# Start addresses of the on-chip buffers in a two-layer grid encoder: column buffers in a pool of their own, constants padded

## The chip, the core and the metric

The kernel runs on one core of a Trainium2 chip. A core has five engines with instruction streams of their own: TensorE (PE; its weight loads are shown as PEld), VectorE (DVE), ScalarE (ACT), GpSimd (POOL) and SyncE (SP), which here issues the transfers. The metric is the device time of one execution in microseconds; lower is better.

## The reference

An encoder trunk of two layers over 512 tokens (a grid of 8 x 64) of 1,024 features, with 256 memory tokens:

```
for l in range(2):
    h = rms_norm(x, norm_mix[l])
    x = x + (even_mixer(h) if l == 0 else odd_mixer(h))
    x = x + memory_cross_attention(rms_norm(x), rms_norm(mem))
    x = x + conv_ffn(rms_norm(x))          # 1024 -> 2 x 2816 -> 1024
```

The even mixer is grouped-query attention and a two-way mLSTM behind one input projection and one output projection; the odd mixer is neighbourhood attention and differential attention in the same form. The feed-forward part projects up, applies a convolution over three positions and a gate, and projects down. Everything is in fp32.

## The kernel before

Activations lie transposed: a tile holds 128 features (rows) by 512 tokens (columns). To keep the precision of fp32 each operand is split into a rounded part and a rest, `hi` and `lo`, both in a rounded fp32 format (fp32r), and a product is made of three matmuls (`mm3`): w_hi x h_hi, w_hi x h_lo, w_lo x h_hi. `gemm` runs these three for each of the eight blocks of 128 features. Weights come in chunks of 128 x 1024: `stage` transfers a chunk into a buffer of class st, and `weights` splits it into a buffer of class w (hi in the first half, lo in the second). In `gemm` the weights are the stationary operand (128 columns) and a tile of activations is the moving one (512 columns). In `tok_gemm`, which makes rows of tokens, it is the other way about: the activations are stationary, and the moving operand is 512 columns of w. Attention products and transposes are in plain fp32.

Instructions are recorded first (`Recorder.add`) and then ordered by a list schedule (`Recorder.schedule`) from costs in the source; it also gives each buffer a slot of its class (`SLOTS`): 80 of class a (512 floats in each partition), 4 of st (1,024), 3 of w (2,048), 48 of c (8 floats: the columns of a few numbers for each partition) and 8 banks p for sums. `Recorder.trace` issues the instructions in that order, which is why nearly every row of the profile names line 391. The schedule knows slots by number only and no addresses.

A slot gets its place in memory when a pool meets its tag for the first time; a pool lays its tiles one behind the other, each at the next multiple of 32 bytes. Constants lie in the pool "const", ahead of the pool "slots", which holds a, st, w and c mixed in the order of their first use. In the program as built:

- The constants ones, ones64, ident, identr and vec start 32 bytes past a multiple of 128, because eps ahead of them takes 4 bytes.
- a0 to a60, all st and all w start 64 bytes past a multiple of 128.
- c0 (32 bytes) was first used after a60 and before a61, and so a61 to a79 start 96 bytes past a multiple of 128. The other c follow at the end.

Within a buffer all matmul operands start at multiples of 512 bytes, so they keep these remainders. 5,419 matmuls are of 512 columns in fp32r: 1,200 of them have a moving operand at 96, all others at 64.

How slot numbers are read: the names below are slot, number of the buffer and number of the instruction that first wrote it. These are TensorE's rows in the middle of one block of the first layer's up projection, destination first, then moving and stationary operand. Of the slots in them a72, a69, a66, a79 are at 96 and a20 and w0 at 64.

```order
L391 MATMUL p1_3121_4153<-a72_2578_3503,w0_3056_4077 128x512
L391 MATMUL p1_3121_4153<-a69_2586_3514,w0_3056_4077 128x512
L391 MATMUL p1_3121_4153<-a72_2578_3503,w0_3056_4077 128x512
L391 MATMUL p1_3121_4153<-a66_2594_3524,w0_3056_4077 128x512
L391 MATMUL p1_3121_4153<-a79_2603_3536,w0_3056_4077 128x512
L391 MATMUL p1_3121_4153<-a66_2594_3524,w0_3056_4077 128x512
L391 MATMUL p1_3121_4153<-a20_2616_3551,w0_3056_4077 128x512
```

The next block begins with a26, a43, a26, a44, a60, a44, a24 against w1, all at 64.

Of the kernel before, what the change touches and what calls it, by code (L numbers as in the profile page):

```python
# [11 lines left out]
F32 = mybir.dt.float32  # L12
# [13 lines left out]
SLOTS = {"a": (80, 512), "st": (4, 1024), "w": (3, 2048), "c": (48, 8), "p": (8, 512)}  # L26
# [24 lines left out]
NVEC = _vec_layout()  # L51


class Buf:
    """A buffer of one slot class; the slot is chosen when the schedule is made."""

# [5 lines left out]
class View:  # L62
    """A recorded view of a Buf; resolved to an access pattern when its instruction is traced."""

# [23 lines left out]
    def grid(self, pattern, i):  # L88
        """[p, n] as [p, i, n/i] ("p (i c) -> p i c") or, of columns in the other order, "p (c i) -> p i c"."""
        p, n = self.dummy.shape  # L90
        return View(self.buf, self.ops + (("grid", (pattern, i)),), np.broadcast_to(np.int8(0), (p, i, n // i)))

    def spread(self, n):
        """[p, m] as [p, m, n], each element n times."""
        p, m = self.dummy.shape
        return View(self.buf, self.ops + (("spread", n),), np.broadcast_to(np.int8(0), (p, m, n)))
# [17 lines left out]
class Op:  # L114
    """An instruction: alts holds (engine, method, args, keywords, cost, latency) for each engine that may run it."""

# [20 lines left out]
class Recorder:  # L137
    """Records instructions with their buffers, orders them by a list schedule, then traces them in that order."""

# [97 lines left out]
    def schedule(self, slots):  # L237
        """List schedule: each engine takes, of the instructions that are ready, the first in program order. A
        buffer is given one of its class's slots with its first write and gives it back after its last use."""
        import heapq  # L240
# [153 lines left out]
class Kern:  # L394
# [33 lines left out]
    def finish(self):  # L428
        tc = self.tc
        pool = lambda name, **kw: self.ctx.enter_context(tc.tile_pool(name=name, bufs=1, **kw))  # L430
        sb, ps = pool("slots"), pool("banks", space=bass.MemoryType.PSUM)
        rec = self.nc
        rec.trace(rec.schedule({c: n for c, (n, w) in SLOTS.items()}),
                  lambda cls: (ps if cls == "p" else sb, SLOTS[cls][1]))

# [11 lines left out]
    def rest(self, lo, src, hi, gain=None, rows=slice(None)):  # L447
        """lo: what scaled_copy's rounding left of src * gain."""
        if gain is None:
            self.nc.vector.tensor_tensor(lo, src, hi.bitcast(F32), op=OP.subtract)  # L450
        else:
            self.nc.vector.scalar_tensor_tensor(lo, src, gain[rows], hi.bitcast(F32), op0=OP.mult, op1=OP.subtract)
# [58 lines left out]
class Norm:  # L511
# [29 lines left out]
    def columns(self):  # L541
        """rstd, and its square, of token 128 * t + p in row p of columns t and 4 + t."""
        K, nt = self.K, self.n // 128
        nc = K.nc
        p = K.ps("t")[:, :32 * nt]
        for t in range(nt):
            nc.tensor.transpose(p[:, 32 * t:32 * t + 32], self.r[0:32, t * 128:t * 128 + 128], K.ident[0:32, 0:32])
        self.rc = K.col("rc")
        nc.vector.tensor_copy(self.rc[:, :nt].grid(ROWS, nt), p.grid(ROWS, nt)[:, :, 0:1])
        nc.vector.tensor_tensor(self.rc[:, 4:4 + nt], self.rc[:, :nt], self.rc[:, :nt], op=OP.mult)  # L550
# [16 lines left out]
def softmax(K, sc, n, bias=None):  # L567
    """exp(sc - max) and 1 / its sum, of sc and of a bias added to it."""
    nc = K.nc
    c = K.col("sm")  # L570
    P = K.a("P")[:, :n]
    if bias is None:
        nc.vector.tensor_reduce(c[:, 0:1], sc, op=OP.max, axis=AX.X, negate=True)
        nc.scalar.activation(P, sc, AF.Exp, bias=c[:, 0:1], accum_out=c[:, 1:2])
    else:
        nc.vector.tensor_tensor_reduce(P, sc, bias, -1.0, 3.0e38, op0=OP.add, op1=OP.min, accum_out=c[:, 0:1])
        nc.scalar.activation(P, P, AF.Exp, bias=c[:, 0:1], scale=-1.0, accum_out=c[:, 1:2])
    nc.vector.reciprocal(c[:, 2:3], c[:, 1:2])
    return P, c[:, 2:3]


class Head:
    """One head, or two (parts) of 64 columns each: score(i, part) -> P of query tile i, finish(Ps) -> P tiles by part,
    v(kt) -> the stationary operands of key block kt by part, take(y)."""

# [71 lines left out]
def merge(main, fill, name, rest=True):  # L657
    """Emit main, with fill's work spread through it (ratio of PE time), and then what is left of fill (rest)."""
    debt, ratio = TUNE[name + "0"], TUNE[name]
    for c in main:  # L660
        debt += c * ratio
        while fill is not None and debt > 0:
            try:
                debt -= next(fill)
            except StopIteration:
                fill = None
        yield c
    if rest and fill is not None:
        yield from fill
# [12 lines left out]
def q_stack(K, q, gain=None):  # L682
    """Two heads' [hi; lo] rows: [qa_hi; qa_lo] and [qb_lo; qb_hi]."""
    lo, hi = slice(0, 64), slice(64, 128)
    qa, qb = K.ar("qa"), K.ar("qb")
    for t, src, dst in ((qa, lo, hi), (qb, hi, lo)):
        K.scaled_copy(t[src], q[src], gain, src)
        K.rest(t[dst], q[src], t[src], gain, src)
    return qa, qb


def k_stack(K, k, gain=None):
    """What the stacked q is multiplied with, of two heads: hi against both its halves, lo against its hi half."""
    nc = K.nc
# [12 lines left out]
def scores2(K, q2, k2, i, keys=None):  # L707
    """Query tile i against all keys, or against two key tiles."""
    nc = K.nc
# [14 lines left out]
def trunk(ctx, tc, xT, memT, vec, lam_in, rope, ev_w, ev_o, od_w, od_o, ca_q, ca_kv, ca_o, up, down, na_u, t5, outT):  # L724
# [3 lines left out]
    real = tc.nc  # L728
    eps = pc.tile([128, 1], F32, name="eps")
    real.vector.memset(eps, EPS)  # L730
# [17 lines left out]
    x, w0 = [], []  # L748
    V, mix = K.const(pc.tile([128, NVEC], F32, name="vec")), K.const(pc.tile([128, 8], F32, name="mix"))
    nc.sync.dma_start(mix, vec[:, :8])  # L750
# [41 lines left out]
    def tok_gemm(w, nrm, width):  # L792
        """Token rows times `width` columns of a matrix: a bank holds 512 // width blocks of 128 tokens."""
        kp, per = 1024 // width, 512 // width
# [18 lines left out]
    class Tok:  # L813
        """Token rows: groups of `width` columns, each a list of banks."""

# [8 lines left out]
    def tok_values(w, nrm, v, roll=False):  # L824
        """Values, each token row times its rstd; roll: row n goes to row n + 64."""
        width, per = v.width, 512 // v.width
# [15 lines left out]
    def tok_norm(w, nrm, width, refine):  # L842
        """Token rows, rms_norm over each head of 64, but for its gain. A list of transposed 128-column chunks."""
        per, nh = 512 // width, width // 64
# [25 lines left out]
    def tok_heads(w, nrm, width, gain, refine, stack, roll=False):  # L870
        """Heads of 64 with their gain, transposed and stacked; roll: token n goes to column n + 64."""
        per = 512 // width
# [22 lines left out]
    def proj_norm(w, m, nrm, ones, gain, n=S, d=64, refine=False):  # L895
        """rms_norm over each head of (h * nrm.r) @ w: scale free but for eps, which becomes eps / nrm.r ** 2.
        refine: a Newton step on the root, which turns its sign; gain is negated for it."""
        p = K.ps("g")[:, :n]
        yield from K.gemm(p, w[m], nrm.hs)
        with nc.boosted("qk"):  # L900
            return norm_bank(p, nrm, ones, gain, n, d, refine)
# [240 lines left out]
    def diff(st, ys):  # L1142
        lm = K.a("lm")
        nc.sync.dma_start(lm[:, 0:256], bass.AP(tensor=lam_in.tensor, offset=lam_in.offset, ap=[[0, 128], [1, 256]]))
        lc = K.const(pc.tile([128, 8], F32, name="lam"))
        for j in range(2):
# [34 lines left out]
    def na(st, ys):  # L1181
        """A tile of 128 tokens is 16 grid columns. Keys are turned by 8 columns, so that the windows of query tile i
        lie in key tiles i and i + 1; the last tile's follows on the first, whose halves are at the grid's two ends."""
        def pair(j):
# [22 lines left out]
    def mem_norm(l):  # L1207
        """The memory times a layer's gain; its rstd is the same for both layers."""
        nm = Norm(K, vcol("mem", 8 * l, 8), 256)
# [247 lines left out]
def _rows(yT):  # L1457
    """The output's columns are tokens in column-major order of the grid."""
    return np.ascontiguousarray(yT.reshape(D, 64, 8).transpose(2, 1, 0)).reshape(1, S, D)
# [15 lines left out]
```

## Time and profile before

| | |
|---|---|
| median of 3 runs | 1453.91 us (1449.54 to 1457.04) |
| span of the profiled execution | 1447.9 us; the profile gives no other time of it |
| PE, matmuls | 1430.4 us busy, 6463 records |
| PE, weight loads | 1130.6 us busy |
| VectorE, ScalarE | 966.4 us, 760.4 us busy |
| queue q1 (all transfers) | 29.3% of 16 engines |

The span runs from the first to the last instruction; the time of a run also holds what lies ahead of it and behind it. A matmul's bar is longer than its share of the time, since matmuls overlap in the array: what one costs is the length of a stretch without gaps, divided by the weight loads in it (one for each matmul).

### The profile page before, as it was taken

To read this page: it belongs to the slowest core of one execution; us is meant where nothing else is said; L and a number is where in the kernel's file an instruction comes from. 1 tells how busy PE (TensorE), PEld (TensorE's weight loads), DVE (VectorE), ACT (ScalarE), POOL (GpSimd) and SP (SyncE) were. 2 spreads that over 40 slices of the span, in tenths; PEclk is the share of its full clock that TensorE was granted. 3 is DMA by queue.
4 is the path that set the end of the run, shared out by engine and by line. 5 is a ranking of instruction groups with operands and counts; after the bars stand their busy time and mean duration, and the time that the engine had idled before them with its cause. 6 is when DMAs were issued, how large, how long until landed. Compare 5 with 4: busy or idle time off the path is not lost. (4 is left out here: it accounts for less than half of the span.)

```text
span 1447.9 us, 17456 instructions
## 1 busy us (share of the span) xinstructions
PE 1430.4 (99%) x6463; PEld 1130.6 (78%) x6463; DVE 966.4 (67%) x1744; ACT 760.4 (53%) x1334; POOL 24.0 (2%) x60
## 2 busy tenths in 40 slices
PE   8999999999999999999999999999999999999998
PEld 5787777786888888888888767877778888888887
DVE  7885587666867776733458797857568777776221
ACT  6575697667444444422346777866754444443111
POOL 0000011000000000000000000000000000000000
PEclk9999999999999999999999999999999999999999
DMA  6221221231232333333252402433213332322421
GB/s 235 73 73 59 66 80 56 79 118 45 88 101 90 100 90 100 88 95 97 86 197 67 138 30 88 154 95 107 76 58 90 100 96 94 99 91 66 142 95 48
DMA packets 48182, 135.70 MB, mean 94 GB/s; under 512 B 5473, under 2 KB 12129, under 8 KB 48097
## 3 DMA queue, kind: packets, MB, share of 16 engines
q1 hardware_dynamic: 48096, 134.60, 29.3%
q8 instruction: 50, 0.82, 0.2%
q14 instruction: 36, 0.29, 0.1%
HBM read 132.48 MB, written 2.10 MB: 93 GB/s over the span
## 5 line engine op out<-in xcount | busy, mean ns | idle before, releaser
L391 PE MATMUL p<-a,w 128*128 128x512 f32 (+1 forms) x4560 | 1067.8, 390 | 0.5 <-DVE w L391 0.5
L391 PEld LDWEIGHTS p<-a,w 128*128 128x128 f32 x4560 | 840.7, 188 | 198.1 <-issue 14.6
L391 DVE TENSOR_TENSOR w<-st,w 128x1024 fp32r<-128x1024 f32 (+2 forms) x246 | 279.3, 1136 | 160.7 <-ACT w L391 160.0
L391 ACT CAST w<-st 128x1024 fp32r<-128x1024 f32 (+2 forms) x219 | 213.6, 977 | 247.9 <-PE p L391 221.8
L391 PE MATMUL p<-w,a 128*128 128x512 f32 x768 | 202.2, 402 | 0.9 <-DVE w L391 0.6
L391 DVE SCALAR_TENSOR_TENSOR a<-a,vec,a 128x504 f32<-128x504 f32 (+3 forms) x324 | 183.3, 590 | 11.6 <-ACT a L391 7.5
L391 DVE TENSOR_TENSOR a<-a,a 128x512 fp32r<-128x512 f32 (+5 forms) x215 | 143.4, 670 | 37.5 <-ACT a L391 34.2
L391 PEld LDWEIGHTS p<-w,a 128*128 128x128 f32 x768 | 140.8, 188 | 35.3 <-issue 5.9
L391 DVE TENSOR_TENSOR a<-p,a 128x512 f32<-128x512 f32 (+2 forms) x127 | 85.4, 673 | 108.3 <-PE p L391 82.2
L391 ACT ACTIVATE a<-a 128x512 f32<-128x512 f32 (+2 forms) x170 | 100.7, 600 | 102.3 <-DVE a L391 101.1
L391 PE MATMUL p<-a,a 128*128 128x512 f32 (+1 forms) x424 | 135.0, 432 | 6.6 <-ACT a L391 5.6
L391 ACT CAST a<-a 128x512 fp32r<-128x512 f32 (+2 forms) x92 | 55.9, 608 | 149.3 <-DVE a L391 148.4
L391 ACT ACTIVATE a<-a,vec 128x512 f32<-128x512 f32 (+2 forms) x139 | 105.8, 764 | 43.0 <-DVE a L391 41.4
L391 ACT ACTIVATE a<-a,c 128x256 f32<-128x256 f32 (+3 forms) x172 | 98.4, 598 | 19.6 <-DVE c L391 19.2
L391 PEld LDWEIGHTS p<-a,a 128*128 128x128 f32 x424 | 76.3, 191 | 31.9 <-ACT a L391 10.0
L391 DVE TENSOR_TENSOR a<-a,p 128x512 f32<-128x512 f32 (+1 forms) x65 | 47.9, 738 | 58.4 <-PE p L391 58.4
L391 PEld LDWEIGHTS p<-ident,a 128*128 128x128 f32 (+2 forms) x474 | 55.5, 140 | 26.4 <-DVE a L391 7.3
L391 PE MATMUL p<-ident,a 128*128 128x128 f32 (+2 forms) x474 | 70.0, 273 | 4.2 <-DVE a L391 3.5
L391 ACT COPY a<-p 128x512 f32<-128x512 f32 (+1 forms) x121 | 61.0, 536 | 18.0 <-PE p L391 17.6
L391 ACT ACTIVATE a<-p,c 128x512 f32<-128x512 f32 (+2 forms) x81 | 48.3, 609 | 24.8 <-DVE c L391 17.0
L391 DVE TENSOR_REDUCE c<-p 128x1 f32<-128x512 f32 (+1 forms) x64 | 34.5, 553 | 13.7 <-PE p L391 12.7
L391 ACT ACTIVATE a<-p 128x512 f32<-128x512 f32 (+1 forms) x58 | 30.9, 533 | 20.3 <-PE p L391 20.1
(73 smaller groups left out, 483.3 us busy)
## 6 DMA issues: line engine op xcount, KB each, us to landing
st<-in_up_dram SPq DMA_DIRECT2D x88, 512.0 KB, 3.5
st<-in_down_dram SPq DMA_DIRECT2D x32, 512.0 KB, 3.6
st<-in_od_w_dram SPq DMA_DIRECT2D x24, 512.0 KB, 4.2
st<-in_ev_w_dram SPq DMA_DIRECT2D x22, 512.0 KB, 3.6
st<-in_ca_kv_dram SPq DMA_DIRECT2D x16, 512.0 KB, 4.4
st<-in_down_dram SPq DMA_DIRECT2D x16, 384.0 KB, 3.2
st<-in_ev_o_dram SPq DMA_DIRECT2D x16, 256.0 KB, 2.5
st<-in_ca_q_dram SPq DMA_DIRECT2D x8, 512.0 KB, 3.5
```

The costliest lines, as they stand in the source:

```text
L391: getattr(getattr(nc, eng), fn)(*[r(v) for v in args], **{k: r(v) for k, v in kw.items()})
```

## The change

Three small tiles among the constants are made 32 floats wide (128 bytes) and used through a view of their old width, vec is rounded up to a multiple of 32 floats, and class c gets a pool "columns" of its own that is opened ahead of "slots". The other lines of the diff take away docstrings.

```
     def finish(self):
         tc = self.tc
         pool = lambda name, **kw: self.ctx.enter_context(tc.tile_pool(name=name, bufs=1, **kw))
-        sb, ps = pool("slots"), pool("banks", space=bass.MemoryType.PSUM)
+        cb, sb, ps = pool("columns"), pool("slots"), pool("banks", space=bass.MemoryType.PSUM)
         rec = self.nc
         rec.trace(rec.schedule({c: n for c, (n, w) in SLOTS.items()}),
-                  lambda cls: (ps if cls == "p" else sb, SLOTS[cls][1]))
+                  lambda cls: ({"p": ps, "c": cb}.get(cls, sb), SLOTS[cls][1]))
...
-    eps = pc.tile([128, 1], F32, name="eps")
+    eps = pc.tile([128, 32], F32, name="eps")[:, 0:1]
...
-    V, mix = K.const(pc.tile([128, NVEC], F32, name="vec")), K.const(pc.tile([128, 8], F32, name="mix"))
+    V, mix = K.const(pc.tile([128, -(-NVEC // 32) * 32], F32, name="vec")), K.const(pc.tile([128, 32], F32, name="mix"))
+    V, mix = V[:, :NVEC], mix[:, :8]
...
-        lc = K.const(pc.tile([128, 8], F32, name="lam"))
+        lc = K.const(pc.tile([128, 32], F32, name="lam"))
```

In the program as built afterwards the 48 columns lie in one block of 1,536 bytes behind the constants, and every constant and every a, st and w starts at a multiple of 128 bytes; a, st and w also start at multiples of 2,048. All engines have the same instructions in the same order as before, on the same slots; only addresses differ. Slots a0 to a60, st and w move up by 1,856 bytes, a61 to a79 by 1,824.

## Rows read from the trace of the kernel before

**Rows 1.** The page, its first part: busy us, share of the span, instructions.

```profile
span 1447.9 us, 17456 instructions
PE 1430.4 (99%) x6463; PEld 1130.6 (78%) x6463; DVE 966.4 (67%) x1744; ACT 760.4 (53%) x1334; POOL 24.0 (2%) x60
```

**Rows 2.** Busy time by stretch of the span; then granted clock, DMA share, GB/s.

```profile
0.00:21.00 21.00, 14.79 (x51) 9.91 (x52) 14.91 (x32) 15.68 (x23) 3.61 (x12) 1.00 0.84 304
21.00:850.00 829.00, 824.60 (x3713) 649.91 (x3713) 567.66 (x994) 454.93 (x791) 20.36 (x48) 1.00 0.29 91
850.00:1054.00 204.00, 200.86 (x1012) 154.05 (x1010) 147.10 (x349) 147.03 (x344) 0.00 (x0) 1.00 0.29 92
1054.00:1444.00 390.00, 389.86 (x1691) 316.73 (x1690) 235.94 (x369) 142.80 (x180) 0.00 (x0) 1.00 0.28 90
```

**Rows 3.** Waits, whole span: us in total, times, longest.

```profile
PE p L391 <- ACT a L391: 6.3, 4, 5.6
PE p L391 <- DVE a L391: 5.7, 9, 1.0
...
PE p L391 <- DVE w L391: 1.1, 2, 0.6
PE p L391 <- DVE c L391: 0.2, 1, 0.2
...
ACT a L391 <- DMA a<-in_xT_dram: 2.9, 2, 2.1
...
ACT w L391 <- DMA st<-in_ev_w_dram: 0.6, 1, 0.6
```

**Rows 4.** The chain that ended last, its last piece: start, us, what.

```profile
1054.21 390.11 PE p L391 x1690
```

**Rows 5.** Stretches of six matmuls: columns as in rows 2, PE, then PEld.

```profile
452.72:454.12 1.40, 1.40 (x8) 1.13 (x6) 1.16 (x2) 0.11 (x1) 0.00 (x0) 1.00 0.51 94
455.73:457.10 1.37, 1.37 (x7) 1.12 (x6) 0.98 (x2) 1.37 (x2) 0.00 (x0) 1.00 0.00 0
```

**Rows 6.** Up projection of the first and of the second layer, columns as in rows 2.

```profile
350.00:580.00 230.00, 230.00 (x997) 186.79 (x996) 168.15 (x216) 104.27 (x133) 0.00 (x0) 1.00 0.30 94
1065.00:1295.00 230.00, 230.00 (x999) 187.22 (x998) 176.53 (x292) 101.93 (x130) 0.00 (x0) 1.00 0.31 96
```

**Rows 7.** Seven plain fp32 records of 256 columns, cross-attention, columns as in rows 2.

```profile
323.25:324.76 1.51, 1.51 (x8) 1.33 (x7) 0.87 (x3) 1.31 (x2) 0.00 (x0) 1.00 0.00 0
```

**Rows 8.** Three runs of token-row matmuls (moving operand in w), columns as in rows 2.

```profile
740.76:750.52 9.76, 9.76 (x45) 8.07 (x43) 2.50 (x3) 1.55 (x2) 0.00 (x0) 1.00 0.38 107
763.13:774.48 11.35, 11.35 (x51) 9.38 (x50) 9.22 (x12) 5.19 (x7) 0.00 (x0) 1.00 0.18 52
787.90:798.34 10.44, 10.44 (x47) 8.63 (x46) 9.97 (x13) 8.60 (x12) 0.00 (x0) 1.00 0.01 2
```

**Rows 9.** The page, DMA queue's share and the commonest issue (KB each, us to landing).

```profile
q1 hardware_dynamic: 48096, 134.60, 29.3%
...
st<-in_up_dram SPq DMA_DIRECT2D x88, 512.0 KB, 3.5
```

**Rows 10.** Waits of SP's own queue: us in total, times, longest.

```profile
SPq L391 <- DVE w L391: 916.7, 181, 26.0
```

## The prediction

> **What bounds the kernel now.** I read the busy shares first. [...] In the two long stretches, 21 to 850 us and 1054 to 1444 us, PE is busy for 824.60 of 829.00 and 389.86 of 390.00 us; only the attention stretch around 850 to 1054 us leaves it some idle time, 3.1 us [rows 2]. The waits say the same: PE's matmuls wait 6.3 us for ScalarE and 7.0 us for VectorE in the whole execution, and the longest waits on a transfer are 2.9 us and 0.6 us, both of ScalarE [rows 3]. The chain that ended last closes with 390.11 us of nothing but 1690 matmuls [rows 4]. So the time is the number of matmuls times what one costs, and the question is what the change does to that cost.
>
> A matmul's own bar (393 ns in the wide stretches) overlaps its neighbours', so I take a stretch and divide by its weight loads, one for each matmul. The last chain gives 390.11 / 1690 = 230.8 ns [rows 4]. [...] All matmuls of this size in rounded fp32 together (5,419 by the order of the program) make 5,419 x 230.8 ns = 1,251 us of the span; each nanosecond on one is 5.4 us.
>
> **What the trace shows of addresses.** Before the change there are three kinds of start: 64 bytes past a multiple of 128 (slots a0 to a60, all st and all w), 96 past (a61 to a79) and 32 past (the constants). No large buffer starts at a multiple of 128, so the trace does not show the new address itself. It shows 64 against 96. In the first layer's up projection six matmuls in a row stream slots a72, a69 and a66, a79, all at 96: 1.40 us for six, 233 ns each. Three microseconds later six in a row stream a43, a26, a44, a60, a24, all at 64: 1.37 us, 228 ns each [rows 5]. Weights and destinations are of one kind in both. Over long stretches the difference is thinner, as it should be: the first layer's up projection, with 10 of 24 matmuls at 96, takes 230.00 us / 996 = 230.9 ns each; the second layer's, with 6 of 24, 230.00 / 998 = 230.5 ns [rows 6]. That is 0.46 ns for a sixth more at 96, or 2.8 ns for one. So an operand at 96 costs 3 to 5 ns more than one at 64.
>
> [...]
>
> **The change part by part.**
>
> Order and counts: all five engines issue the same instructions in the same order on the same slots, and the layout stays below the top of the memory. Nothing is added, removed or made to wait, and no instruction passes another on any queue, SP's and POOL's included. Cost 0.
>
> Large buffers from 96 to a multiple of 128: 1,200 of the 5,419 matmuls stream such a buffer. If a multiple of 128 is as good as 64, each loses 3 to 5 ns: 3.6 to 6.0 us; I take 4 ns, 4.8 us. All of it is on PE, so it counts in full.
>
> Large buffers from 64 to a multiple of 128 (4,219 matmuls): not shown. One bound is 0, if what counts is a half of 128 bytes. [...] I take 0, from a row that lies nearer: three runs of 43, 50 and 46 matmuls of token rows, which stream w (at 64), hold 227.0 ns for one (9.76 / 43, 11.35 / 50, 10.44 / 46) [rows 8], whatever weights they load. A steady figure with no jitter looks like a fixed price of this kind of matmul rather than a start that falls badly; the stretches at 230.5 lie only 3.5 ns above it. [...]
>
> Constants from 32 to a multiple of 128: they are weights of some hundred matmuls and the operand of the transposes. At 3 ns each this is under half a microsecond.
>
> Transfers: staged rows now start at multiples of 128. A 512 KB transfer lands in 3.5 us, and the queue is busy for 29.3% [rows 9]; SP's queue itself mostly waits for a slot to be given back (916.7 us on VectorE's w) [rows 10]. [...]
>
> VectorE and ScalarE: their waits are on PE or on each other, and both have a third of the time free [rows 1]. Should the address move their durations by a few per cent, PE would hide it.
>
> Sum: 1447.9 - 4.8 = 1443.1 us of span. The profile gives no time of its execution beside the span; the median of the runs shown, 1453.9 us, lies 6.0 above it, and I carry these 6.0 over: **1449 us**, 0.3% less. From no change a measurement of this kernel tells about 0.5%, 7 us; so the likeliest outcome is one that looks like none. Its own range is 1442 to 1455 us: what is left of the 96-class at 3 to 5 ns, and about 0.2% up or down because the slots' pairs fall differently (228 against 233 ns shows how far one row of pairs can lie from another).
>
> **The rivals.**
>
> [...]
>
> (b) A second step of the size of the first: from 64 to 128 gains once more what 96 to 64 gains, 3 to 5 ns on all. With 4 ns: 5,419 x 4 + 1,200 x 4 = 26 us, 1428 us. For it: that such a step exists at all. Against it: nothing shows a third level.
>
> (c) Slower: every buffer now starts at the same offset within 2 KB blocks, weights and moving operand alike, and the streams meet more often. The price is the gap between the two sixes: if all stretches went to the 233 ns of the slower, 5,419 x 2.2 = 12 us, 1466 us. It decides from 1.3 ns on one matmul (7 us). Against it: in the stretches of [rows 8] weights and moving operand already share their offset, and these are the fastest.
>
> (d) Nothing at all, 1454 us: the 96-class is slow for what lies high in the memory, not for its start, since a61 to a79 are also the highest slots. [...]
>
> **How the numbers follow.** The forecast 0.36, (d) 0.12, (a) 0.20, (b) 0.18, (c) 0.14. A sixth of the forecast falls beyond -0.5%, and a sixth of (b) falls short of it. Faster by over 0.5%: 0.20 + 0.15 + 0.06 = 0.41. Slower by over 0.5%: 0.10 of (c). Within: 0.49. Range: below, (a) has too much to be left out, so it reaches to 1372 (the full 82 us); above, 1460 leaves out the worse half of (c).
>
> **What would show it.** Right: the stretch of six at a72, a69, a66, a79 falls to about 229 ns, the runs on w stay at 227, the last chain goes from 230.8 to 229 or 230 ns for one, and the up projections of both layers cost the same. (a): the runs on w fall to 216. (b): they fall to 223. (c): they rise, and the waits stay as they are. I am wrong in the main step if the runs on w move by more than 2 ns, since that is where I set the unseen step from 64 to 128 at nothing.

## The result, and the profile after

The changed kernel takes 1436.63 us, the median of 4 runs (1434.39 to 1438.35), against 1451.72 us for the kernel before in the same comparison: a ratio of 0.9892, interval 0.9874 to 0.991. That is 1.1% or 15 us less. The forecast was 1449 us and no difference that can be told; the sign was right, the size three times too small. The measured time lies outside the forecast's own 1442 to 1455 us, and inside the whole range only because that was drawn down to 1372 us for (a), by 82 us that no run shows: that part is luck.

The page's first part, after the change, answers to [rows 1]:

```profile
span 1434.2 us, 17456 instructions
PE 1416.3 (99%) x6463; PEld 1132.6 (79%) x6463; DVE 965.8 (67%) x1744; ACT 761.6 (53%) x1334; POOL 24.1 (2%) x60
```

The span is 13.7 us shorter, PE's busy time 14.1 us; VectorE and ScalarE are as busy as they were. PE's waits for them, in the view of waits (us in total, times, longest), answer to [rows 3]:

```profile
PE p L391 <- ACT a L391: 6.7, 5, 5.5
PE p L391 <- DVE a L391: 5.7, 9, 1.0
...
PE p L391 <- DVE w L391: 1.1, 2, 0.6
```

So nothing waits less. The gain lies in the matmuls, and the last piece of the chain that ended last shows it at once, beside [rows 4] (start, us, what):

```profile
1046.85 383.77 PE p L391 x1690
```

The same 1690 matmuls take 6.34 us less, 227.1 ns each instead of 230.8. Busy time by stretch (columns as in rows 2) has, in this order: the start; the up projections of both layers, beside [rows 6]; the two stretches of six, beside [rows 5]; the three runs on w, beside [rows 8].

```profile
0.00:21.00 21.00, 14.96 (x46) 10.85 (x47) 13.17 (x30) 13.61 (x21) 3.61 (x12) 1.00 0.82 304
...
350.00:580.00 230.00, 230.00 (x1016) 190.44 (x1015) 171.65 (x220) 107.55 (x136) 0.00 (x0) 1.00 0.31 96
1065.00:1295.00 230.00, 230.00 (x1016) 190.50 (x1016) 178.92 (x297) 103.05 (x132) 0.00 (x0) 1.00 0.32 97
...
451.12:452.48 1.36, 1.36 (x7) 1.13 (x6) 1.21 (x2) 0.02 (x1) 0.00 (x0) 1.00 0.36 51
454.07:455.43 1.36, 1.36 (x7) 1.13 (x6) 0.96 (x2) 1.36 (x2) 0.00 (x0) 1.00 0.00 0
...
734.20:743.97 9.77, 9.77 (x45) 8.07 (x43) 2.50 (x3) 1.54 (x2) 0.00 (x0) 1.00 0.34 107
756.49:767.83 11.34, 11.34 (x52) 9.38 (x50) 9.22 (x12) 5.19 (x7) 0.00 (x0) 1.00 0.18 51
781.20:791.62 10.42, 10.42 (x47) 8.64 (x46) 9.96 (x13) 8.59 (x12) 0.00 (x0) 1.00 0.01 2
```

Both up projections now do about 1,016 matmuls in 230 us, 226.4 to 226.6 ns each. Both stretches of six take 1.36 us, 226.7 ns: the one that streamed a72, a69, a66, a79 fell by 6 ns, and the one that was taken as undisturbed fell too, from 228. The runs on w did not move (227.2, 226.8, 226.5 ns). The granted clock is 1.00 in all of these stretches, as before, so the clock gave nothing.

Both programs issue the same matmuls in the same order, so the time from one start to the next can be read from both traces and compared one by one. By part of the span of before: +2.0 us in the first 21 us (46 matmuls done instead of 51, [rows 2]), -1.7 from 21 to 340, -6.8 from 340 to 735, -0.5 to 850, -0.3 to 1054, and -6.3 to the end; together -13.6. By kind, for rounded matmuls of 512 columns that follow one another, leaving out intervals of 250 ns or more in either trace (gaps):

```
moving operand before         matmuls   before     after      in all
a61 to a79 (96 mod 128)       1,173     233.2 ns   226.9 ns   -7.3 us
a0 to a60  (64 mod 128)       3,261     229.6 ns   227.2 ns   -7.9 us
w          (64 mod 128)         654     229.8 ns   228.4 ns   -0.9 us
```

These three make -16.1 us; all other intervals together, the gaps among them, are 2.5 us longer, and 2.1 of these lie in the first 21 us. The buffers at 64, whose share the prediction set at nothing, gave half. The time lost at the start does not follow the addresses: among the kernels below that are as fast as this one, the first 21 us hold from 44 matmuls (experiment 11) to 50 (3 and 9), in one profiled execution each.

### The profile page after: what moved, and what is told of

Same layout as the page of the kernel before. It is cut to its first block, busy times and chain, and to the rows that moved or that the text cites. A ratio compares the mean times of both kernels' runs of the same rounds, so it can differ in the third digit from the quotient of the medians.

```text
span 1434.2 us, 17456 instructions
## 1 busy us (share of the span) xinstructions
PE 1416.3 (99%) x6463; PEld 1132.6 (79%) x6463; DVE 965.8 (67%) x1744; ACT 761.6 (53%) x1334; POOL 24.1 (2%) x60
## 5 line engine op out<-in xcount | busy, mean ns | idle before, releaser
L391 PE MATMUL p<-a,w 128*128 128x512 f32 (+1 forms) x4560 | 1053.1, 387 | 0.5 <-DVE w L391 0.5
```

The costliest lines, as they stand in the source:

```text
L391: getattr(getattr(nc, eng), fn)(*[r(v) for v in args], **{k: r(v) for k, v in kw.items()})
```

## The experiments

No kernel here leaves out any work, and the schedule's instructions and their order stay the same in all; only addresses differ. Where an edit adds a filler tile, one small memset is added. The theories at first: **class** (a start at 64 or 96 past a multiple of 128 costs, a multiple of 128 does not), **likeness** (what costs is that buffers start differently from each other), **height** (the slots a61 to a79 are slow because they lie high), and **constants**.

**1. The columns' pool alone.** The kernel before, with this hunk of the change and no padding. Then a, st and w all start 64 past a multiple of 128.

```
-        sb, ps = pool("slots"), pool("banks", space=bass.MemoryType.PSUM)
+        cb, sb, ps = pool("columns"), pool("slots"), pool("banks", space=bass.MemoryType.PSUM)
...
-                  lambda cls: (ps if cls == "p" else sb, SLOTS[cls][1]))
+                  lambda cls: ({"p": ps, "c": cb}.get(cls, sb), SLOTS[cls][1]))
```

> The pool for the columns alone, constants left at 32 past a multiple of 128: all a, st and w then start 64 bytes past one, a61 to a79 too. Theory 64 (only the place within 64 bytes counts): as fast as the change, 1437 us, 226.7 ns for one matmul of the last chain. Theory 128 (multiples of 128 are needed): only what the slots at 96 cost goes away, some 6 us, so 1446 us and 229.5 to 230 ns. Theory of the mixture (operands that start at different places within 128 bytes disturb each other, whatever the place): 1437 us.

1436.34 us against 1451.98; ratio 0.9883, 0.9868 to 0.9898: the whole gain, with not one large buffer at a multiple of 128. First layer's up projection (columns as in rows 2):

```profile
350.00:580.00 230.00, 230.00 (x1016) 190.51 (x1015) 171.64 (x220) 107.54 (x136) 0.00 (x0) 1.00 0.31 96
```

The slots a61 to a79 still lie highest, so height is out as well. The class theory is out as far as it says that 64 is worse than 0.

**2. The padding alone.** The changed kernel with c left in "slots". Then a0 to a60, st and w start at multiples of 128, a61 to a79 32 past one.

```
-        cb, sb, ps = pool("columns"), pool("slots"), pool("banks", space=bass.MemoryType.PSUM)
+        sb, ps = pool("slots"), pool("banks", space=bass.MemoryType.PSUM)
...
-                  lambda cls: ({"p": ps, "c": cb}.get(cls, sb), SLOTS[cls][1]))
+                  lambda cls: (ps if cls == "p" else sb, SLOTS[cls][1]))
```

> The padded constants alone, columns still among the other slots: a0 to a60, st and w start at multiples of 128, a61 to a79 at 32 past one. Theories 64 and 128: only the 1,200 matmuls with a moving operand in a61 to a79 lose 6 to 7 ns, 7 to 8 us over the change, 1445 us. Theory of the mixture: pairs of unlike slots disturb each other on both sides, 1449 us or more.

1451.57 us against 1451.98; ratio 0.9997, 0.9987 to 1.0006: no change. The same stretches as in [rows 6] and [rows 5]:

```profile
350.00:580.00 230.00, 230.00 (x997) 186.90 (x996) 167.60 (x214) 104.65 (x134) 0.00 (x0) 1.00 0.30 94
...
454.12:455.52 1.40, 1.40 (x8) 1.12 (x6) 1.16 (x2) 0.11 (x1) 0.00 (x0) 1.00 0.61 70
457.13:458.50 1.37, 1.37 (x7) 1.13 (x6) 0.98 (x2) 1.37 (x2) 0.00 (x0) 1.00 0.00 0
```

996 matmuls, 1.40 and 1.37 us, and a last piece of 390.11 us: figure for figure the kernel before, though the two remainders are 0 and 32 where they were 64 and 96. What the two kernels share is the 32 bytes between a60 and a61. The constants, padded here, give nothing that can be measured.

**3 and 4. All at another place.** The changed kernel with a wider constant behind which everything moves: by 32 bytes (a, st, w at 32 past a multiple of 128) and by 128 (at 128 past a multiple of 2,048).

```
-        lc = K.const(pc.tile([128, 32], F32, name="lam"))
+        lc = K.const(pc.tile([128, 40], F32, name="lam"))      # 3;  64 in 4
```

> The change with 32 bytes more in the last constant: all a, st and w start 32 bytes past a multiple of 128. Theories 64 and 128: every matmul pays as the class at 96 did before, 233 ns, 6.3 ns over the change on 5,419 matmuls, 34 us, 1471 us. Theory of the mixture: all are alike, 1437 us.

> The change with 128 bytes more in the last constant: all a, st and w start at multiples of 128, but 128 past a multiple of 2,048, and so each runs over the end of a block of 2 KB. Theory of the 2 KB block (a buffer must not run over its end): between before and the change, 1445 to 1452 us. Theories 64, 128 and the mixture: as the change, 1437 us.

1435.91 us, ratio 0.989 (0.9871 to 0.9908), and 1438.89 us, 0.9901 (0.9884 to 0.9919), against 1451.98. At the four places tried with all large buffers alike (0 in the change, 32 and 128 here, 192 in experiment 1, each modulo 256) the matmuls cost the same: the last piece takes 383.77 us, in experiment 4 383.78. This is the up projection of the first layer with all at 32:

```profile
350.00:580.00 230.00, 230.00 (x1017) 190.41 (x1016) 171.93 (x220) 107.20 (x135) 0.00 (x0) 1.00 0.30 96
```

**5, 6, 9 and 10. How far apart?** Only likeness was left. A filler of n bytes is put ahead of a61 in the changed kernel, so that a61 to a79 start n bytes off the remainder of all others.

```
+    padded = False
...
                 pool, width = home(b.cls)
+                if b.cls == "a" and b.slot == 61 and not self.padded:
+                    self.padded = True
+                    nc.vector.memset(pool.tile([128, 32], F32, name="pad"), 0.0)   # 128 bytes; 16, 64, 128 for 64, 256, 512
```

> The change, with a tile of 128 bytes laid ahead of a61: a0 to a60, st and w start at multiples of 2,048, a61 to a79 at 128 past one; all are multiples of 128. Theory of the mixture within 128 bytes: all are alike, 1437 us and 227 ns for one. Theory of any mixture (slots must be whole multiples of their size apart): as before, 1451 us, 230.4 ns.

> The same with a tile of 64 bytes: a61 to a79 start 64 past a multiple of 128, the others at one. If the mixture counts within 64 bytes: 1437 us. If within 128 bytes: 1451 us or, if twice the distance costs twice, up to 1465 us.

> As e5 and e6, with a tile of 256 bytes ahead of a61. If what counts is the distance of two starts within some block, this run and the next find the block. Block of 256 bytes: 1437 us, 227 ns. Block of 512 bytes or more: slower than that, 1443 to 1451 us, as e5 with 128 bytes (1446.7 us, 229.3 ns).

> The same with 512 bytes. The weights in w start at multiples of 512 bytes of one another already, and the change shows no jitter among them, so a block of 512 bytes gives 1437 us, 227 ns. If the block is 2,048 bytes, the size of a slot: 1443 to 1451 us.

```
apart     median us   before     ratio, interval
64        1453.40     1451.86    1.0017  1.0005 to 1.0029
128       1446.68     1451.86    0.9961  0.9946 to 0.9976
256       1434.34     1451.44    0.9881  0.9857 to 0.9905
512       1435.49     1451.44    0.9884  0.9864 to 0.9904
```

At 128 bytes apart, all starts are multiples of 128, which is what the change brings about in words, and two thirds of its gain are gone; the time lies between the two that were expected. At 256 and 512 nothing is lost. Up projections of the first and second layer with 128 apart:

```profile
350.00:580.00 230.00, 230.00 (x998) 187.04 (x998) 167.80 (x215) 104.84 (x135) 0.00 (x0) 1.00 0.31 94
1065.00:1295.00 230.00, 230.00 (x1009) 188.76 (x1008) 178.56 (x295) 103.56 (x132) 0.00 (x0) 1.00 0.31 96
```

with 64 apart:

```profile
350.00:580.00 230.00, 230.00 (x1000) 187.49 (x999) 168.09 (x215) 105.02 (x134) 0.00 (x0) 1.00 0.30 94
1065.00:1295.00 230.00, 230.00 (x992) 186.06 (x991) 175.71 (x289) 102.01 (x131) 0.00 (x0) 1.00 0.30 94
```

and with 256 apart, first layer:

```profile
350.00:580.00 230.00, 230.00 (x1016) 190.47 (x1015) 171.91 (x220) 107.06 (x135) 0.00 (x0) 1.00 0.31 96
```

The unlike buffers make up 10 of 24 moving operands in the first layer and 6 of 24 in the second; at 128 apart the price follows that (230.5 and 228.2 ns), at 64 it does not (230.2 and 232.1).

In these runs and in 2 the slots a61 to a79 lie off the weights too, so the times alone do not tell moving against moving from moving against stationary. The trace of 6 does: in the projections a matmul whose moving operand lies like its weights, but whose forerunner streamed one 64 off, averages 234.3 ns (780 of them), while one that is 64 off its weights behind another such averages 230.9 ns (318). At 32 (the kernel before) and at 128 (5) the unlike one pays more: 233.1 and 233.0 ns behind a like one, against 229.7 and 227.5 ns for the like one behind it.

**7, 8 and 11. Weights against the moving operand.** The buffers of class w get a pool of their own ahead of a filler tile and the slots, so that all a are alike and all w are alike, but not a and w.

```
-        cb, sb, ps = pool("columns"), pool("slots"), pool("banks", space=bass.MemoryType.PSUM)
+        cb, wb, pb, sb, ps = pool("columns"), pool("wide"), pool("pad"), pool("slots"), pool("banks", space=bass.MemoryType.PSUM)
+        pad = pb.tile([128, 16], F32, name="pad")         # 7: w at 0, a and st at 64
+        tc.nc.vector.memset(pad, 0.0)
...
-                  lambda cls: ({"p": ps, "c": cb}.get(cls, sb), SLOTS[cls][1]))
+                  lambda cls: ({"p": ps, "c": cb, "w": wb}.get(cls, sb), SLOTS[cls][1]))
```

In 8 the filler has 24 floats and lam 40 (w at 32, a and st at a multiple of 128); in 11 the filler has 64 (w at 0, a and st 256 off). The expectations below speak of 32 bytes in 8, which holds modulo 128. In the program as built a and st of 8 start 128 past a multiple of 256 and w 32 past one, so modulo 256, the block that 9 to 11 point to, they are 96 apart.

> The change with a pool of its own for w, at multiples of 128, and a and st all at 64 past one: moving operands are all alike, but the stationary ones of the projections start elsewhere. If only moving operands among each other count: 1437 us, 227 ns. If moving against stationary counts too: every matmul of the projections is slow, 230 to 233 ns, 1451 to 1465 us.

> The same with w at 32 past a multiple of 128 and a and st at multiples of 128, the distance of 32 that e2 had among moving operands. If only moving operands among each other count: 1437 us. If moving against stationary counts too: 1451 to 1465 us.

> w in a pool of its own at multiples of 2,048, a and st at 256 past one. If the block is 256 bytes: 1437 us, 226.7 ns. If it is larger: all projections pay, as with 64 bytes (1446.9 us) and 32 bytes (1465.3 us). [...]

```
apart     median us   before     ratio, interval
64        1446.89     1451.86    0.9958  0.9941 to 0.9974
96        1465.26     1451.86    1.0090  1.0075 to 1.0105
256       1435.97     1451.44    0.9892  0.9871 to 0.9912
```

64 costs less than was expected of it (1451 us or more). The same modulus again, now between the operand that streams and the one that is loaded. The rows below are the first layer's up projection and the first run on w (the same 43 matmuls as in [rows 8]). With w and a 64 apart:

```profile
350.00:580.00 230.00, 230.00 (x1006) 188.73 (x1005) 168.76 (x216) 106.06 (x135) 0.00 (x0) 1.00 0.31 94
...
740.52:750.55 10.03, 10.03 (x44) 8.08 (x43) 2.49 (x3) 1.54 (x2) 0.00 (x0) 1.00 0.34 105
```

with 96 apart:

```profile
350.00:580.00 230.00, 230.00 (x988) 184.93 (x987) 165.75 (x213) 102.94 (x133) 0.00 (x0) 1.00 0.29 92
...
749.47:759.55 10.08, 10.08 (x45) 8.10 (x43) 2.50 (x3) 1.55 (x2) 0.00 (x0) 1.00 0.32 106
```

with 256 apart:

```profile
350.00:580.00 230.00, 230.00 (x1016) 190.47 (x1015) 171.58 (x220) 107.57 (x137) 0.00 (x0) 1.00 0.31 96
...
734.64:744.41 9.77, 9.77 (x44) 8.07 (x43) 2.50 (x3) 1.53 (x2) 0.00 (x0) 1.00 0.35 109
```

A matmul of the up projection costs 228.9, 233.0 and 226.6 ns, one of the run on w 233.3, 234.4 and 227.2. Weights 32 off a steady moving operand are seen in the kernel before: in its projections matmuls at 96 behind another at 96 average 233.2 ns (318). There too, of the matmuls that stream w, the 164 whose own or next stationary slot lies at 96 fell from 232.4 to 228.4 ns with the change, the 441 with both at 64 only from 228.7 to 228.4. The last piece of the chain says it over 1690 matmuls (rows with 64, 96 and 256 apart):

```profile
1055.34 387.43 PE p L391 x1690
```

```profile
1065.33 394.87 PE p L391 x1690
```

```profile
1047.26 383.77 PE p L391 x1690
```

So the place of w against a changes a matmul's pace in these kernels: 394.87 us with 96 apart against 383.77 with 256 apart, for the same matmuls.

No version beats the change: 1, 3, 4, 9, 10 and 11 equal it within their intervals.

## Why the prediction was right or wrong

**What held.** PE is the bound from end to end (busy for 99% of the span before and after) and the price of one matmul is the whole matter; order, waits and transfers add nothing; VectorE and ScalarE hardly move (966.4 and 760.4 us of work before, 965.8 and 761.6 after); the constants give nothing (experiment 2). The commonest transfer lands in 3.5 us after the change as before. Two readings were off without weight: the 2.9 us of ScalarE on a transfer are the sum of two waits [rows 3], and ScalarE has not a third but nearly half of its time free [rows 1]. The stretch of six fell as foreseen, but further; both up projections now cost the same; the runs on w stayed.

**The step that failed** is the one on the large buffers at 64: "I take 0" for 4,219 matmuls, from [rows 8]. Those on a moving a gave 7.9 us. And the term for the 1,200 at 96 was too small: 233.2 fell to 226.9 ns, 6.3 for each instead of 4, 7.3 us instead of 4.8. Both have one origin. The prediction asked how each start lies against 128 bytes, and so took the buffers at 64 as the undisturbed kind and 228 ns in [rows 5] as their price. At the four places tried with all large buffers alike no start was better or worse by itself (experiments 1, 3, 4 and the change: 383.77 or 383.78 us for the last piece). In the experiments rounded matmuls were slow when the starts of operands read near one another in time differed modulo 256 bytes. For one of the first layer's up projection: slots 32, 64 and 128 apart, 230.9, 230.2 and 230.5 ns (2, 6, 5); 256 and 512 apart, 226.6 (9, 10); weights 64 and 96 off the moving operand, 228.9 and 233.0; 256 off, 226.6 (7, 8, 11); all alike, 226.4 to 226.6. Before, a61 to a79 lay 32 bytes off both the other slots and w, by c0, and so runs of matmuls that changed between the two groups of slots lost on both. Other distances were not tried; that the block is 256 is an inference from 256 and 512 being free and 128 not.

A smaller part of the miss is the base. The 6.0 us carried over from span to time were mostly not overhead: every run whose span is on record takes about 1.7 us more than its span, and the rest is that the execution profiled was faster than the median of three. That median, 1453.9 us, was 1451.7 in the later comparison. So about 2 of the 12 us between forecast and result are base and 10 are gain (15 us instead of 4.8).

**The evidence was there and was misread.** The runs on w in [rows 8] have w as moving operand and slots of a0 to a60 as stationary one, all at one remainder. The prediction noted this against rival (c), and yet used the same rows to show that 64 costs what a multiple of 128 costs. They showed the price of like operands. Its test of itself (the main step is wrong if the runs on w move by more than 2 ns) could not fail for that reason: they stayed, and the step was wrong. Experiment 7 moves those 43 matmuls from 9.77 to 10.03 us by making w and a unlike, with every a still in one class.

**Why the buffers at 64 lost too** is read from the trace before and not tested by itself. In the projections matmuls at 64 whose neighbours on both sides are at 64 too averaged 229.7 ns before and 227.1 ns after the change (1,849 of them). Sorted by how many matmuls ago the moving operand last changed its remainder, clean intervals average 231.5 ns at the change (1,697 of them), 231.4 one later (477), 227.0 nine later (81), 226.9 ten later (70); in between they don't fall evenly (228.8 at three, 232.7 at five). So the disturbance seems to outlast the change by several matmuls, and most buffers at 64 stand close to one at 96. With the columns' pool no change of remainder among these buffers is left, and no such loss.

**The rivals.** No run shows the 82 us for which (a) set the low end of the range: the fastest long stretches of rounded matmuls, under any alignment tried, hold 226.4 ns for one, and the runs on w, which (a) put at 216, stayed between 226.5 and 227.2 wherever the operands were alike. Nor do the seven plain fp32 records of [rows 7] follow the addresses: moving a66 and stationary a46 lie 32 apart before and alike after, and they take 1.51 us both times, 215.7 ns each.

```profile
323.53:325.04 1.51, 1.51 (x8) 1.32 (x7) 0.87 (x3) 1.31 (x2) 0.00 (x0) 1.00 0.00 0
```

(b) comes nearest by its time, but there is no step from 64 to 128: all at 64 (experiment 1) is as fast as the change. (c) had the two facts that matter, that weights and moving operand share their offset and that they do so in the fast runs on w, and turned them round: meeting at one offset is the fast case, and experiment 8, with w and a 96 bytes apart modulo 256, gives 1465 us and 233.0 ns where (c) feared 1466 and 233. (d) is false: a61 to a79 lie as high as before and are fast.

**Open.** Why 128 apart costs (1446.68 us) and 256 and 512 do not (1434.34 and 1435.49), no run shows. Nor is it known why weights 64 off the moving operand cost less (228.9) than 96 off (233.0), while with 19 of 80 slots off 64 is the dearest distance tried (1453.40 us; 1451.57 at 32, 1446.68 at 128). In the changed kernel 8% of the clean intervals (428 of 5,093) still take over 230 ns: about 1% of those in the two feed-forward stretches, 18 to 31% of those in the others behind the first 21 us. Their cause was not tried.

## What to carry to other kernels

Where rounded fp32 matmuls bound a kernel as they do this one, print the start addresses of all its operands modulo 256 and try them alike: one 32-byte tile in the middle of a pool of large slots cost 1.1% here, and a pool of its own for small tiles was the whole cure without any padding (ratio 0.9883 in experiment 1, 0.9892 for the change). Before choosing an undisturbed stretch as the base of an estimate, write down every property in which it differs from the rest, not only the one under test: the runs on w differed from the others in likeness as well as in class. And when a change is named for one property (multiples of 128), try the other that it brings along (all alike) by shifting everything at once.

## What the runs showed of the hardware that was not expected

- Rounded fp32 matmuls of 512 columns took 226.4 to 227.2 ns for one in the up projections, the last piece and the runs on w shown, when their operands were alike modulo 256 bytes, at each place tried (a multiple of 2,048 bytes, 32 or 64 past one of 128, 128 past one of 2,048). Elsewhere 18 to 31% of the clean intervals took over 230 ns all the same (see Open). The seven plain fp32 records of [rows 7] took 1.51 us both times, unlike and alike.
- With weights and moving operand 96 bytes apart modulo 256 a matmul of the up projection cost 233.0 ns, at 64 228.9; on w as moving operand 234.4 and 233.3. At 256 these were 226.6 and 227.2, so the place of the weights changed the pace of the matmuls here.
- A change of remainder among moving operands cost more in experiment 6 than a steady difference from the weights in 7: with 6 of 24 at 64 apart, 232.1 ns (second layer), with all 64 off the weights, 228.9 to 229.2 (up projection and last piece).
